# Small products set singly between 512-column products, fillers at the start, and spatial weights fetched behind VectorE

## The chip, the cores and the metric

The kernel runs on one core of one Trainium2 chip. Its metric is device time in microseconds (us), the median of several executions. A core has TensorE (PE, the 128x128 matmul array, which writes to PSUM), VectorE (DVE), ScalarE (ACT), GpSimd (POOL) and SyncE (SP); here SP and POOL mostly issue DMAs, each in the order of its queue. A PE product is two steps, a weight load (PEld: the stationary operand, 128 columns here) and the matmul (the moving operand, up to 512 columns). A transpose is a product with the identity.

## The reference, cut to what matters

```python
# SEQ 256, D 2048, two layers, all float32; rms_norm before every sub-layer, plain residual adds
z = gelu(h @ w_in); u, v = split(z)                      # layer 0: spatial gating, chunks of 128 tokens
v = rms_norm(v, g_v).reshape(..., CHUNK, 16 heads, 128)
s = einsum('hts,bcshd->bcthd', tril(w_s), v) + b_s
h = h + (u * s) @ w_out
u = h @ w_in                                             # layer 1: S5, 128 heads of 16 channels, 64 states
x_t = abar * x_{t-1} + bbar @ u_t                        # complex diagonal scan over the chunk
y = c @ x (real part) + d * u
ga, gb = split(gelu(y) @ w_glu); h = h + ga * sigmoid(gb)
# after each of the two: gated MLP, hidden 5632
z = causal_conv3(h @ w_up) + conv_b; gate, val = split(z)
h = h + (silu(gate) * val) @ w_down
```

## The kernel before, in words

All 256 tokens stay on chip: `hn` holds the residual stream, and the weights (about 400 MB) are streamed once. Each weight tile (1 MB) comes by a DMA of SP into one of three raw buffers. ACT rounds it to a high part (`wh`, L124), DVE takes the difference (`wl`, L125), and the activations are split in the same way, so that each fp32 product is made of three: high by high, high by low, low by high. Each of them is 512 columns wide in the two forms that hold most of the work, `group_b` (L893 to L895, into `accb`) and `form_b` (L987 to L989, into `accv`). `form_a` makes a pair of 512 and 256 columns (L786 and L787, into `acc`).

Between these stand small products of 128 columns or less, all on PE:
- `stage_pair` (L821, `pt`): four transposes bring a pair of 128-channel chunks of the residual into `X`, the moving or stationary operand of the next layer. `residual` and `glu_evac` put such calls on a list, `pending`, and `drain` takes one from it after each weight tile.
- `activate` in the gated MLP (L916, `zt`): four transposes per chunk of 128 hidden units, then convolution, silu and product on ACT and DVE, into `Gt`. These calls go through `pending` too; there are 88 of them, 352 transposes.
- `spatial_weights` (L1089, `ps_w`) and `spatial` (L1108, `ps_s`) in the spatial gating; `wr` and `bb_` are the spatial weights and biases, loaded by POOL (L1084, L1086).
- S5 (16 groups of heads): `drive` (L584, `ps_x`), then the rotation by a table (`tab`, loaded by SP, doubled by ACT at L566), the scan and the rotation back on ACT and DVE, then `outputs` (`ps_y`: 4 products at L639 from the input, 8 at L645 from the scan's result `sp`), `gelu` on ACT (L653, `y`). One step of each is issued after each weight tile, in an order by slots (`sched`, `step`).
- The preparation of S5's constants runs in the background of the first gated MLP, some instructions after each tile (`bg`, `ps_k` at L458).

These products go through two PSUM buffers of one pool (`misc`). At the start PE runs 7 products of ones (`warm`, L1041) while the input comes.

A scheduler of the language lays the program's instructions out on the engines, by a modelled timeline: it may move an instruction behind later ones of its engine. So the order on PE is not quite the order of the code. `issue_after(ins)` is a context that keeps the instructions issued in it behind `ins` on `ins`'s engine.

Of the kernel before, what the change touches and what calls it, by code (L numbers as in the profile page):

```python
# [66 lines left out]

N_WARM = 7

BG_OUT = (1.0, 1.0, 1.0, 0)  # L70
# [446 lines left out]
class S5Tokens:  # L517
# [61 lines left out]
    def drive(self, s):  # L579

        st = self.st[s]
        st["x"] = self.psum.tile([P, 512], F32, name=f"ps_x{s}", tag="misc")
        for i in range(4):
            self.nc.tensor.matmul(  # L584
                st["x"][:, i * P : (i + 1) * P], st["pw"][:, i, :], st["ubd"][:, i, :], start=True, stop=True
            )

    def take(self, s):
# [80 lines left out]
def tile_hybrid_trunk(  # L669
# [101 lines left out]
    def form_a_steps(Xt, nks, blocks, evac, k0=0):  # L771

        pairs = [acc_ps.tile([P, 2, 512], F32, name="acc", tag="acc") for _ in range(len(blocks) // 2)]
        k_first, ktot = k0, k0 + sum(nks)
        for nk in nks:
            part = ws.get()  # L780
            for b, c0 in enumerate(blocks):
                ps = pairs[b // 2][:, b % 2, :]
                for kk in range(nk):
                    k = k0 + kk
                    wh, wl = part(kk, c0, P)
                    T.matmul(ps, wh, Xt[k], start=k == k_first, stop=False, skip_group_check=True)  # L786
                    T.matmul(ps[:, NT:], wl, Xt[k][:, :NT], start=False, stop=k == ktot - 1, skip_group_check=True)  # L787
                if k0 + nk == ktot and b % 2 == 1:
                    evac(b // 2, pairs[b // 2])
            k0 += nk  # L790
            yield
# [19 lines left out]

    def stage_pair(i, g_col, pool=None):

        if pool is None:
            pt = misc_ps.tile([P, 512], F32, name="pt", tag="misc")
        else:
            pt = pool.tile([P, 2, 512], F32, name="pt", tag="acc")[:, 0, :]
        for j in range(2):
            for a in range(2):
                c = 2 * i + j  # L820
                T.transpose(pt[:, j * NT + a * P : j * NT + (a + 1) * P], hn[:, a, c * P : (c + 1) * P], ident)  # L821
        for j in range(2):
            stage_x(2 * i + j, g_col, pt[:, j * NT : (j + 1) * NT])
# [24 lines left out]
    rb2 = bcast(rbc, 2, 1)  # L848
    pending = []

    def drain(n=1):

        while pending and n > 0:
            pending.pop(0)()
            n -= 1

    def residual(tp, g, ps, g_col=None):
# [3 lines left out]
        if g_col is not None:  # L861
            for a in range(2):
                square_sum(tp, hv[:, a, :], nss[:, a, g : g + 1])
            for i in (2 * g, 2 * g + 1):
                pending.append(lambda i=i: stage_pair(i, g_col))
            if g == 3:
# [11 lines left out]
    def group_b_steps(Xt, nks, evac, after=None, k0=0):  # L878
# [6 lines left out]
        for ti, nk in enumerate(nks):  # L885
            part = ws.get()
            for kk in range(nk):
                k = k0 + kk
                wh, wl = part(kk, 0, 512)
                for tt in range(2):  # L890
# [3 lines left out]
                    T.matmul(ps[:, tt, :], xh, wl, start=False, stop=False)  # L894
                    T.matmul(ps[:, tt, :], xl, wh, start=False, stop=k == ktot - 1)  # L895
            k0 += nk
            if k0 == ktot:
                evac(ps)
            drain()
            if after is not None and ti in after:  # L900
# [7 lines left out]
    def ffn(l, g_next, fin=None):  # L908
        cw = conv

        def activate(z, c, q, k):

            pt = misc_ps.tile([P, 512], F32, name="zt", tag="misc")
            for v in range(2):
                for tt in range(2):
                    T.transpose(  # L916
                        pt[:, v * NT + tt * P : v * NT + (tt + 1) * P],
                        z[:, tt, v * NT + q * P : v * NT + (q + 1) * P], ident,
                    )
            a = fpool.tile([P, 2, NT], F32, name="a", tag="a", bufs=2)  # L920
            for v in range(2):
# [55 lines left out]
    def form_b_steps(Xt, nks, pss, own=0, between=None):  # L977
# [15 lines left out]
        for k, (get, kk) in enumerate(chunks):  # L993
            part = get() if get else part
            w = part(kk, 0, 512)
            product(k, w, 0)
            if k < ktot - own:
                product(k, w, 1)
            else:
                kept.append((k, w))  # L1000
# [7 lines left out]
    with ExitStack() as sgu_ctx:  # L1008
# [35 lines left out]
        stage_pair(0, cols[:, 0], acc_ps)  # L1044
        ws.split(0)
        stage_pair(1, cols[:, 0], acc_ps)
        pss = acc_ps.tile([P, 2, 512], F32, name="accv", tag="acc")
        first_v = form_b_steps(X, [4] * 4, [pss[:, tt, :] for tt in range(2)])
        for i in range(2, 8):
            stage_pair(i, cols[:, 0])  # L1050
# [7 lines left out]
        total_r(vss, 4, rtok)  # L1058


        for g in range(4):
# [17 lines left out]
        for g in range(4):  # L1079
            st = {}  # L1080

            def spatial_weights(g=g, st=st):
                wr = sp.tile([P, 4, P], F32, name="wr", tag="wr", bufs=2)
                nc.gpsimd.dma_start(wr, a_w_s[0][4 * g : 4 * g + 4].rearrange("h t s -> t h s"))  # L1084
                st["b"] = sp.tile([P, 4, P], F32, name="bb_", tag="bb_", bufs=2)
                nc.gpsimd.dma_start(st["b"], dram(a_b_s, g * 512, [[0, P], [1, 512]]).rearrange("p (h t) -> p h t", h=4))  # L1086
                ps = misc_ps.tile([P, 512], F32, name="ps_w", tag="misc")
                for i in range(4):
                    T.transpose(ps[:, i * P : (i + 1) * P], wr[:, i, :], ident)  # L1089
                w = st["w"] = sp.tile([P, 4, P], F32, name="wst", tag="wst", bufs=2)  # L1090
                A.copy(w.rearrange("s h t -> s (h t)"), ps)
# [11 lines left out]
            def spatial(p, st=st, g=g):  # L1103
                ps = misc_ps.tile([P, 512], F32, name="ps_s", tag="misc")
                for i in range(2):
                    hd = 4 * g + 2 * p + i
                    for a in range(2):
                        T.matmul(  # L1108
                            ps[:, i * NT + a * P : i * NT + (a + 1) * P],
                            vn[:, a, hd * P : (hd + 1) * P], st["w"][:, 2 * p + i, :], start=True, stop=True,  # L1110
                        )
                s = sp.tile([P, 2, 2, P], F32, name="s_", tag="s_", bufs=3)
                for i in range(2):
# [17 lines left out]
            def first(g=g):  # L1131
                if g == 0:
                    make_rbc(sp)
                spatial_weights()
# [26 lines left out]
    with tc.tile_pool(name="s5", bufs=1) as sp:  # L1161
# [17 lines left out]
        for s in range(KC):  # L1179
            n = N_OF[s]  # L1180
            at(n - 1, s5.load, s)
            at(n - 1, s5.load1, s)
            at(n, s5.drive, s)
            at(n + 1, s5.take, s)
# [7 lines left out]
        order = (  # L1192
            s5.gelu, s5.take, s5.finish, s5.fetch, s5.turn, s5.scan, s5.outputs, s5.drive, s5.load2, s5.load, s5.load1
        )

        n_slot = [0]

        def step():
            for fn, a in sorted(sched.pop(n_slot[0], []), key=lambda e: order.index(e[0])):
                fn(*a)  # L1200
# [32 lines left out]
        def glu_evac(i):  # L1233
            def evac(ps):
                for a in range(2):
# [6 lines left out]
                    square_sum(sp, hv, nss[:, a, i // 2 : i // 2 + 1])  # L1242
                pending.append(lambda: stage_pair(i // 2, cols[:, 3]))
                if i == KC - 2:
# [12 lines left out]
        for i in range(4, KC, 2):  # L1257
            group_b(Ys, [4, 4], glu_keep(i), {0: step, 1: step})
        assert not sched
        craw = fetch_conv(sp, 1)  # L1260
# [71 lines left out]
```

## Time and profile before

| | |
|---|---|
| time, median of 3 runs | 2111.91 us (2110.3 to 2114.04) |
| the profiled execution: its own time, its span | 2112.45 us, 2110.7 us |
| PE busy, weight loads busy | 2092.9 us (99%), 1734.2 us (82%) |
| DVE, ACT, POOL busy | 1438.0, 1151.5, 90.4 us |
| mean granted clock of TensorE | 0.998 |
| HBM read | 410.47 MB, 205 GB/s over the span |

The span runs from the first to the last instruction. Rows of PE's products are as long as the product is in flight; products overlap, so what one costs is the step from its start to the next one's. The stages on the time axis: spatial gating to 200 us, its out-projection and the first gated MLP to about 1050, S5 with the GLU to about 1390, the second gated MLP to the end.

### The profile page before, as it was taken

The page shows a single profiled execution, that of the slowest core. Times are in us where ns is not written, and L with a number is a line of the kernel's source. Part 1 is how long each engine was busy: PE and PEld are TensorE (multiplying, and loading weights), DVE is VectorE, ACT ScalarE, POOL GpSimd, SP SyncE. Part 2 cuts the span into 40 slices and gives each one's busy share as a digit, 9 for nine tenths or more (in the row PEclk, how much of TensorE's full clock was granted, in tenths as well). Part 3 has the DMA queues.
Part 4 walks back from the last instruction along what each step waited for, and adds up shares of the span by engine and source line. Part 5 has one row for each costly group of instructions (what it writes and reads, how often), then busy time and mean ns, then how long its engine had stood idle before and what let it go on. Part 6 is the DMA issues. An engine that isn't in the chain of part 4 may idle for free.

```text
span 2110.7 us, 27318 instructions
## 1 busy us (share of the span) xinstructions
PE 2092.9 (99%) x10279; PEld 1734.2 (82%) x10279; DVE 1438.0 (68%) x2123; ACT 1151.5 (55%) x1672; POOL 90.4 (4%) x142
## 2 busy tenths in 40 slices
PE   9999999999999999999999999999999999999998
PEld 7888888888887788888887788888888888888886
DVE  5476777886896644888779867765655666546565
ACT  6544455554555544555468756555544555345553
POOL 1010000000111110000000000000000000000000
PEclk9999999999999999999999999999999999999999
DMA  8655556666777766666789976565556555555553
GB/s 280 198 185 179 183 191 207 210 228 222 220 236 236 222 215 192 192 205 205 232 251 273 280 220 208 189 202 185 182 191 200 180 189 187 188 194 182 192 185 120
DMA packets 356293, 434.39 MB, mean 206 GB/s; under 512 B 31457, under 2 KB 275265, under 8 KB 355521
## 3 DMA queue, kind: packets, MB, share of 16 engines
q1 hardware_dynamic: 346704, 403.75, 59.9%
q0 software_dynamic: 9424, 28.88, 4.6%
q8 instruction: 81, 1.33, 0.3%
q14 instruction: 52, 0.42, 0.1%
q10 hardware_dynamic: 32, 0.01, 0.0%
HBM read 410.47 MB, written 22.02 MB: 205 GB/s over the span
## 4 chain that ended last, share of the span: by engine, by line
PE 90%; DMA 4%; DVE 3%; issue 2%; ACT 1%; SPq 0%; ACTq 0%; POOL 0%; DVEq 0%; POOLq 0%
PE accb L893 25%; PE accb L894 25%; PE accb L895 25%; PE acc L786 3%; PE zt L916 2%; PE acc L787 1%; PE accv L987 1%; PE accv L988 1%; PE accv L989 1%; DMA tab<-rd 1%; DVE wl L125 1%; DMA yt<-yd 1%; PE pt L821 1%; DMA qd<-qt 1%; DMA yd<-y 1%
## 5 line engine op out<-in xcount | busy, mean ns | idle before, releaser
L125 DVE TENSOR_TENSOR wl<-w,wh 128x1024 fp32r<-128x1024 f32 (+1 forms) x721 | 878.6, 1222 | 571.2 <-ACT wh L124 567.2
L124 ACT CAST wh<-w 128x1024 fp32r<-128x1024 f32 (+1 forms) x721 | 753.9, 1050 | 704.0 <-PE accb L895 606.1
L895 PE MATMUL accb<-wh,X 128*128 128x512 f32 x1408 | 552.3, 392 | 0.0
L893 PE MATMUL accb<-wh,X 128*128 128x512 f32 x1408 | 551.7, 392 | 0.0
L894 PE MATMUL accb<-wl,X 128*128 128x512 f32 x1408 | 549.1, 390 | 0.0
L893 PE MATMUL accb<-wh,Gt 128*128 128x512 f32 x1060 | 415.7, 392 | 0.0
L894 PE MATMUL accb<-wl,Gt 128*128 128x512 f32 x1060 | 413.6, 391 | 0.7 <-DVE wl L125 0.7
L895 PE MATMUL accb<-wh,Gt 128*128 128x512 f32 x1060 | 413.8, 391 | 0.0
L895 PEld LDWEIGHTS accb<-wh,X 128*128 128x128 f32 x1408 | 264.3, 188 | 57.0
L894 PEld LDWEIGHTS accb<-wl,X 128*128 128x128 f32 x1408 | 264.5, 188 | 54.5
L893 PEld LDWEIGHTS accb<-wh,X 128*128 128x128 f32 x1408 | 264.4, 188 | 53.8
L894 PEld LDWEIGHTS accb<-wl,Gt 128*128 128x128 f32 x1060 | 199.1, 188 | 42.0 <-DVE wl L125 1.1
L893 PEld LDWEIGHTS accb<-wh,Gt 128*128 128x128 f32 x1060 | 199.0, 188 | 41.9 <-issue 0.3
L895 PEld LDWEIGHTS accb<-wh,Gt 128*128 128x128 f32 x1060 | 199.0, 188 | 41.4
L786 PE MATMUL acc<-X,wh 128*128 128x512 f32 x512 | 184.6, 402 | 0.0
L787 PE MATMUL acc<-X,wl 128*128 128x256 f32 x512 | 144.9, 283 | 0.0
L786 PEld LDWEIGHTS acc<-X,wh 128*128 128x128 f32 x512 | 96.5, 189 | 22.6 <-issue 0.9
L924 ACT ACTIVATE a<-zt,conv 128x256 f32<-128x256 f32 x176 | 94.3, 557 | 14.9 <-PE zt L916 8.1
L787 PEld LDWEIGHTS acc<-X,wl 128*128 128x128 f32 x512 | 97.1, 190 | 0.6 <-issue 0.2
L943 ACT ACTIVATE z<-accb,rtok 128x512 f32<-128x512 f32 x88 | 55.8, 685 | 65.9 <-PE accb L895 65.9
L925 DVE SCALAR_TENSOR_TENSOR a<-zt,conv,a 128x255 f32<-128x255 f32 x176 | 77.7, 476 | 13.7 <-ACT a L924 13.7
L928 DVE SCALAR_TENSOR_TENSOR a<-zt,conv,a 128x254 f32<-128x254 f32 x176 | 77.1, 474 | 0.7
(300 smaller groups left out, 1423.8 us busy)
## 6 DMA issues: line engine op xcount, KB each, us to landing
w<-in_f_w_up_dram SPq DMA_DIRECT2D x352, 512.0 KB, 4.6
w<-in_f_w_down_dram SPq DMA_DIRECT2D x80, 1024.0 KB, 5.2
w<-in_b_w_glu_dram SPq DMA_DIRECT2D x64, 512.0 KB, 4.8
w<-in_a_w_in_dram SPq DMA_DIRECT2D x28, 1024.0 KB, 5.2
w<-in_a_w_out_dram SPq DMA_DIRECT2D x16, 1024.0 KB, 5.1
w<-in_b_w_in_dram SPq DMA_DIRECT2D x16, 1024.0 KB, 6.5
w<-in_f_w_down_dram SPq DMA_DIRECT2D x16, 512.0 KB, 3.7
qd<-qt POOLq DMA_DIRECT2D x16, 320.0 KB, 5.2
```

The costliest lines, as they stand in the source:

```text
L124: self.nc.scalar.copy(hi[:, a:b], raw[:, o + a : o + b])
L125: self.nc.vector.tensor_tensor(lo[:, a:b], raw[:, o + a : o + b], hi[:, a:b].bitcast(F32), op=ALU.subtract)
L786: T.matmul(ps, wh, Xt[k], start=k == k_first, stop=False, skip_group_check=True)
L787: T.matmul(ps[:, NT:], wl, Xt[k][:, :NT], start=False, stop=k == ktot - 1, skip_group_check=True)
L893: T.matmul(ps[:, tt, :], xh, wh, start=k == k_first, stop=False)
L894: T.matmul(ps[:, tt, :], xh, wl, start=False, stop=False)
L895: T.matmul(ps[:, tt, :], xl, wh, start=False, stop=k == ktot - 1)
L916: T.transpose(pt[:, v * NT + tt * P : v * NT + (tt + 1) * P], z[:, tt, v * NT + q * P : v * NT + (q + 1) * P], ident,)
L924: A.activation(a[:, v], zt, AF.Identity, bias=cw[:, 3, cv : cv + 1], scale=cw[:, 2, cv : cv + 1])
L925: V.scalar_tensor_tensor(a[:, v, 1:], zt[:, : NT - 1], cw[:, 1, cv : cv + 1], a[:, v, 1:], ALU.mult, ALU.add)
L928: V.scalar_tensor_tensor(a[:, v, 2:], zt[:, : NT - 2], cw[:, 0, cv : cv + 1], a[:, v, 2:], ALU.mult, ALU.add)
L943: A.mul(z[:, tt], ps[:, tt], rtok[:, tt : tt + 1])
```

## The change

`activate`, `stage_pair`, `spatial_weights`, `spatial` and `drive` become generators that yield after each small product. `weave` puts such a generator on a list, and `tick`, called after each three products of 512 columns (in `form_b` twice, in `form_a` after each pair), runs it to its next yield. `settle` runs all that is on the list. `drain` is replaced in `group_b` by `resume`, which weaves one pending call, ahead of `evac`. Six products of ones (N_BRIDGE) are set between the first and the second group of the input's transposes. The spatial weights' loads of groups 0 and 1 move to the loop before, under `issue_after(last_on_vector())`.

```diff
+N_BRIDGE = 6
@@ drive
                 st["x"][:, i * P : (i + 1) * P], st["pw"][:, i, :], st["ubd"][:, i, :], start=True, stop=True
             )
+            yield
@@ form_a_steps
                     T.matmul(ps[:, NT:], wl, Xt[k][:, :NT], start=False, stop=k == ktot - 1, skip_group_check=True)
+                    tick()
@@ stage_pair
-    def stage_pair(i, g_col, pool=None):
+    def stage_pair(*args):
+        for _ in stage_pair_steps(*args):
+            pass
+
+    def stage_pair_steps(i, g_col, pool=None):
...
                 T.transpose(pt[:, j * NT + a * P : j * NT + (a + 1) * P], hn[:, a, c * P : (c + 1) * P], ident)
+                yield
@@ 
-    pending = []
+    pending, woven = [], []
+
+    def weave(steps):
+
+        woven.append(steps)
+
+    def tick():
+
+        while woven:
+            if next(woven[0], woven) is not woven:
+                return
+            woven.pop(0)
+
+    def settle():
+        while woven:
+            tick()
 
     def drain(n=1):
 
+        settle()
         while pending and n > 0:
-            pending.pop(0)()
+            for _ in pending.pop(0)():
+                pass
             n -= 1
+
+    def resume():
+
+        settle()
+        if pending:
+            weave(pending.pop(0)())
@@ group_b_steps
                     T.matmul(ps[:, tt, :], xl, wh, start=False, stop=k == ktot - 1)
+                    tick()
             k0 += nk
+            resume()
             if k0 == ktot:
                 evac(ps)
-            drain()
@@ activate
                         z[:, tt, v * NT + q * P : v * NT + (q + 1) * P], ident,
                     )
+                    yield
@@ form_b_steps
             product(k, w, 0)
+            tick()
+            tick()
@@ the start
         ws.split(0)
+        with tc.issue_after(next(i for i in reversed(nc.cur_bb.bb.instructions) if i.engine == mybir.EngineType.PE)):
+            for i in range(N_BRIDGE):
+                T.matmul(warm[:, :P], ones, ones, start=True, stop=True)
         stage_pair(1, cols[:, 0], acc_ps)
...
+        def fetch_spatial(g):
+            st = spatial_of[g]
+            st["wr"] = sp.tile([P, 4, P], F32, name="wr", tag="wr", bufs=2)
+            nc.gpsimd.dma_start(st["wr"], a_w_s[0][4 * g : 4 * g + 4].rearrange("h t s -> t h s"))
+            st["b"] = sp.tile([P, 4, P], F32, name="bb_", tag="bb_", bufs=2)
+            nc.gpsimd.dma_start(st["b"], dram(a_b_s, g * 512, [[0, P], [1, 512]]).rearrange("p (h t) -> p h t", h=4))
...
+            if g > 1:
+                with tc.issue_after(last_on_vector()):
+                    fetch_spatial(g - 2)
...
-                {0: first, 1: lambda: spatial(0), 2: lambda: spatial(1)},
+                {
+                    0: first, 1: lambda: (settle(), weave(spatial(0))),
+                    2: lambda: (settle(), weave(spatial(1))),
+                },
@@ S5
+        def drive(s):
+            weave(s5.drive(s))
...
         def step():
+            settle()
```

How this lays out the instructions, at three places. First PE in an up-projection of the first gated MLP; `zt` are the transposes, `accb` the 512-column products. Before:

```order
L893 MATMUL accb<-wh_3135,X_2036 128x512
L894 MATMUL accb<-wl_3136,X_2036 128x512
L916 MATMUL zt<-ident,z 128x128
L895 MATMUL accb<-wh_3135,X_2036 128x512
L916 MATMUL zt<-ident,z 128x128 x7
L893 MATMUL accb<-wh_3139,X_2182 128x512
L894 MATMUL accb<-wl_3140,X_2182 128x512
```

Now:

```order
L949 MATMUL zt<-ident,z 128x128
L925 MATMUL accb<-wh_2961,X_2255 128x512
L926 MATMUL accb<-wl_2962,X_2255 128x512
L927 MATMUL accb<-wh_2961,X_2255 128x512
L949 MATMUL zt<-ident,z 128x128
L925 MATMUL accb<-wh_2961,X_2258 128x512
L926 MATMUL accb<-wl_2962,X_2258 128x512
L927 MATMUL accb<-wh_2961,X_2258 128x512
L949 MATMUL zt<-ident,z 128x128
```

Eight transposes of two chunks stood together, but for one product; now each stands alone behind three products, in two runs of four. In the whole program 325 of the 352 stand so, where 43 stood alone before.

Second, S5. PE before, at the fifth group's outputs (`ps_y`; its fp32 products run as two passes each, so the trace counts twice as many):

```order
L639 MATMUL ps_y_9810<-ubd_8918,tw_9633 64x128 x4
L786 MATMUL acc<-X_8408,wh_9647 128x512
L787 MATMUL acc<-X_8408,wl_9648 128x256
L786 MATMUL acc<-X_8411,wh_9647 128x512
L787 MATMUL acc<-X_8411,wl_9648 128x256
L786 MATMUL acc<-X_8450,wh_9647 128x512
L787 MATMUL acc<-X_8450,wl_9648 128x256
L786 MATMUL acc<-X_8453,wh_9647 128x512
L787 MATMUL acc<-X_8453,wl_9648 128x256
L786 MATMUL acc<-X_8581,wh_9737 128x512
L645 MATMUL ps_y_9810<-sp_8926,qw_9631 64x64 x8
```

and now:

```order
L642 MATMUL ps_y_9816<-ubd_8913,tw_9634 64x128 x4
L648 MATMUL ps_y_9816<-sp_8921,qw_9632 64x64 x8
L789 MATMUL acc<-X_8471,wh_9648 128x512
L790 MATMUL acc<-X_8471,wl_9649 128x256
L586 MATMUL ps_x_9854<-ubd_8919,pw_9733 128x128
L789 MATMUL acc<-X_8474,wh_9648 128x512
L790 MATMUL acc<-X_8474,wl_9649 128x256
L586 MATMUL ps_x_9854<-ubd_8919,pw_9733 128x128
```

The two parts of ps_y stood apart in 10 of the 16 groups and do so in 2 now; ps_x stands singly. SP there, around the table load of group 6, before and now:

```order
L551 DMA ubd_8922<-ud 64x4x64 x2
L108 DMA w_9651<-in_b_w_in_dram 128x8x256
L574 DMA qw_9631<-qd 128x640
L556 DMA pw_9732<-pd 128x4x128
L655 DMA yd<-y_9685 64x4x64 x2
L565 DMA tab_9639<-rd 64x2x512
```

```order
L553 DMA ubd_8917<-ud 64x4x64
L576 DMA qw_9632<-qd 128x640
L553 DMA ubd_8917<-ud 64x4x64
L567 DMA tab_9640<-rd 64x2x512
L110 DMA w_9652<-in_b_w_in_dram 128x8x256
L658 DMA yd<-y_9691 64x4x64 x2
```

The table's load stood behind the weight tile's and the output's (`yd`), which waits for ACT's `y`; now it stands ahead of both.

Third, POOL at the start, with the semaphores that a row waits for. Before, and now:

```order
L1054 DMA gains<-in_a_g_v_dram 16x128
L1084 DMA wr<-in_a_w_s_dram 128x4x128
L1086 DMA bb__936<-in_a_b_s_dram 128x512
L1084 DMA wr<-in_a_w_s_dram 128x4x128
L1086 DMA bb__1161<-in_a_b_s_dram 128x512
L963 DMA craw_717<-in_f_conv_w_dram 88x3x128 [waits DMASW0_49,Activation_49]
```

```order
L1094 DMA gains<-in_a_g_v_dram 16x128
L1106 DMA wr<-in_a_w_s_dram 128x4x128
L1108 DMA bb__725<-in_a_b_s_dram 128x512
L1106 DMA wr<-in_a_w_s_dram 128x4x128
L1108 DMA bb__881<-in_a_b_s_dram 128x512
L997 DMA craw_727<-in_f_conv_w_dram 88x3x128 [waits DMASW0_49,Activation_49]
```

The spatial weights' loads keep their place, and none of the four waits for a semaphore.

## Rows read from the trace of the kernel before

**Rows 1.** The page's first part: busy time, share of the span, instructions.
```profile
PE 2092.9 (99%) x10279; PEld 1734.2 (82%) x10279; DVE 1438.0 (68%) x2123; ACT 1151.5 (55%) x1672; POOL 90.4 (4%) x142
```

**Rows 2.** Timeline of PE, 317.2 to 322.7 us: start, duration, operation, count.
```profile
317.25 0.39 PE L895 MATMUL accb<-wh,X 128*128 128x512 f32 x1
...
318.38 0.40 PE L894 MATMUL accb<-wl,X 128*128 128x512 f32 x1
318.62 0.27 PE L916 MATMUL zt<-ident,z 128*128 128x128 f32 x1
318.65 0.48 PE L895 MATMUL accb<-wh,X 128*128 128x512 f32 x1
318.97 0.93 PE L916 MATMUL zt<-ident,z 128*128 128x128 f32 x7
...
322.69 0.39 PE L894 MATMUL accb<-wl,X 128*128 128x512 f32 x1
```

**Rows 3.** Timeline of PE, 347.6 to 351.5 us.
```profile
347.61 0.40 PE L894 MATMUL accb<-wl,X 128*128 128x512 f32 x1
347.84 0.60 PE L916 MATMUL zt<-ident,z 128*128 128x128 f32 x4
...
351.50 0.39 PE L894 MATMUL accb<-wl,X 128*128 128x512 f32 x1
```

**Rows 4.** Timeline of PE, 1302.8 to 1304.2 us.
```profile
1302.86 0.39 PE L895 MATMUL accb<-wh,Gt 128*128 128x512 f32 x1
1303.09 0.27 PE L821 MATMUL pt<-ident,hn 128*128 128x128 f32 x1
1303.11 0.48 PE L893 MATMUL accb<-wh,Gt 128*128 128x512 f32 x1
...
1303.89 0.40 PE L893 MATMUL accb<-wh,Gt 128*128 128x512 f32 x1
1304.13 0.40 PE L894 MATMUL accb<-wl,Gt 128*128 128x512 f32 x1
```

**Rows 5.** Two stretches: busy time per engine, granted clock, DMA share, GB/s.
```profile
1100.00:1170.00 70.00, 67.10 (x506) 54.83 (x502) 64.35 (x88) 56.20 (x81) 3.78 (x7) 0.98 0.98 273
1133.20:1136.60 3.40, 3.40 (x24) 2.59 (x23) 1.53 (x2) 1.14 (x2) 0.00 (x0) 0.50 1.07 362
```

**Rows 6.** Timeline of the start, PE, its weight loads (PEld) and POOL.
```profile
1.20 3.06 PEld L1041 LDWEIGHTS warm<-ones 128*128 128x128 f32 x14 [1.20 <-POOL ones L733]
...
3.83 0.80 POOL L1084 DMA_DIRECT2D wr<-in_a_w_s_dram  x1
...
7.74 1.12 PE L821 MATMUL pt<-ident,hn 128*128 128x128 f32 x4 [1.92 <-DMA hn<-in_x_dram]
...
11.21 0.63 PE L987 MATMUL accv<-wh,X 128*128 128x512 f32 x1
...
11.64 0.63 PE L988 MATMUL accv<-wl,X 128*128 128x512 f32 x1
```

**Rows 7.** Timeline of PE in S5, 1181.1 to 1183.7 and 1209.0 to 1210.8 us.
```profile
1181.16 0.39 PE L894 MATMUL accb<-wl,Gt 128*128 128x512 f32 x1
1181.48 0.69 PE L645 MATMUL ps_y<-sp,qw 128*64 128x64 f32 x16
...
1182.76 0.66 PE L639 MATMUL ps_y<-ubd,tw 128*64 128x128 f32 x8
...
1183.68 0.40 PE L895 MATMUL accb<-wh,Gt 128*128 128x512 f32 x1
...
1209.06 0.39 PE L895 MATMUL accb<-wh,Gt 128*128 128x512 f32 x1
1209.38 0.66 PE L639 MATMUL ps_y<-ubd,tw 128*64 128x128 f32 x8
1209.87 0.64 PE L645 MATMUL ps_y<-sp,qw 128*64 128x64 f32 x16
...
1210.77 0.39 PE L894 MATMUL accb<-wl,Gt 128*128 128x512 f32 x1
```

**Rows 8.** Timeline of ACT, 1130 to 1132 us.
```profile
1130.60 1.04 ACT L566 COPY tab<-tab 64x1024 f32<-64x1024 f32 x1 [2.80 <-DMA tab<-rd]
1131.67 0.38 ACT L653 ACTIVATE y<-ps_y 128x256 f32<-128x256 f32 x1
```

More of the change, by code (lines that the diff above doesn't have):

```diff
@@ L864, in residual @@
             for i in (2 * g, 2 * g + 1):
-                pending.append(lambda i=i: stage_pair(i, g_col))
+                pending.append(lambda i=i: stage_pair_steps(i, g_col))
             if g == 3:
@@ L1049, in tile_hybrid_trunk @@
         for i in range(2, 8):
-            stage_pair(i, cols[:, 0])
+            weave(stage_pair_steps(i, cols[:, 0]))
             next(first_v)
             next(first_v)
+            settle()
         for i, src in enumerate((norm_ffn_g[0], norm_mix_g[1], norm_ffn_g[1], a_g_v[0])):
@@ L1058, in tile_hybrid_trunk @@
         total_r(vss, 4, rtok)
+        spatial_of = [{} for _ in range(4)]
+        def fetch_spatial(g):
[4 more added lines that the diff above has]
+            nc.gpsimd.dma_start(st["b"], dram(a_b_s, g * 512, [[0, P], [1, 512]]).rearrange("p (h t) -> p h t", h=4))
         for g in range(4):
@@ L1079, in tile_hybrid_trunk @@
         for g in range(4):
-            st = {}
+            st = spatial_of[g]
             def spatial_weights(g=g, st=st):
[L1083 to L1086, printed above, removed]
+                if g > 1:
+                    fetch_spatial(g)
+                wr = st["wr"]
                 ps = misc_ps.tile([P, 512], F32, name="ps_w", tag="misc")
@@ L1089, in spatial_weights @@
                     T.transpose(ps[:, i * P : (i + 1) * P], wr[:, i, :], ident)
+                    yield
                 w = st["w"] = sp.tile([P, 4, P], F32, name="wst", tag="wst", bufs=2)
@@ L1111, in spatial @@
                         )
+                        yield
                 s = sp.tile([P, 2, 2, P], F32, name="s_", tag="s_", bufs=3)
@@ L1133, in first @@
                     make_rbc(sp)
-                spatial_weights()
+                weave(spatial_weights())
                 scale_v()
@@ L1182, in tile_hybrid_trunk @@
             at(n - 1, s5.load1, s)
-            at(n, s5.drive, s)
+            at(n, drive, s)
             at(n + 1, s5.take, s)
@@ L1192, in tile_hybrid_trunk @@
         order = (
-            s5.gelu, s5.take, s5.finish, s5.fetch, s5.turn, s5.scan, s5.outputs, s5.drive, s5.load2, s5.load, s5.load1
+            s5.gelu, s5.take, s5.finish, s5.fetch, s5.turn, s5.scan, s5.outputs, drive, s5.load2, s5.load, s5.load1
         )
@@ L1198, in step @@
         def step():
+            settle()
             for fn, a in sorted(sched.pop(n_slot[0], []), key=lambda e: order.index(e[0])):
@@ L1242, in evac @@
                     square_sum(sp, hv, nss[:, a, i // 2 : i // 2 + 1])
-                pending.append(lambda: stage_pair(i // 2, cols[:, 3]))
+                pending.append(lambda: stage_pair_steps(i // 2, cols[:, 3]))
                 if i == KC - 2:
@@ L1258, in tile_hybrid_trunk @@
             group_b(Ys, [4, 4], glu_keep(i), {0: step, 1: step})
+        settle()
         assert not sched
```

## The prediction

> **What bounds the kernel now.** I read the busy shares first, then the waits by stretch, then TensorE's (PE's) queue product by product where the change touches it. PE's matmul row is busy 99% of the span [rows 1], so the only things worth counting are what one instruction more or less costs in PE's queue, and the few places where PE does not run. Undisturbed, 512-column products start 0.2267 us apart: five of them lie between 317.25 and 318.38 us [rows 2]. A row's printed length (0.39) is longer than that step because the products overlap; the step between starts is the price.
>
> PE's stops are few. At the start it waits 1.92 us for the input, and until about 13.6 us products start 0.43 apart (11.21 to 11.64) instead of 0.23: TensorE's lower level, 1.2 of 2.4 GHz [rows 6]. In the S5 stage, between 1100 and 1170 us, PE is busy 67.1 of 70 us, VectorE (DVE) 64.35 of 70, and the DMA share is 0.98; for 3.4 us of it the granted clock is 0.50 [rows 5]. Everywhere else PE's own order is the time.
>
> **Part 1: transposes singly.** What does a 128-column transpose cost in a group and alone? Subtract 0.2267 for each 512-column product in a stretch; the rest is the transposes' price, with all they do to the products behind them.
> - Eight, as one, a product and seven [rows 2]: from 318.38 to 322.69 us is 4.31 us and holds 15 products, 3.40. The rest is 0.91, so 0.114 each, or 0.455 for four.
> - Four in a row [rows 3]: from 347.61 to 351.50 us is 3.89 us with 15 products. The rest is 0.49, so 0.12 each.
> - One alone [rows 4], the only clean one: from 1302.86 to 1303.89 us is 1.03 us with 4 products, 0.907. The rest is 0.123. Read one product further, to 1304.13, it is 1.27 less 5 products, 0.137.
>
> So one alone isn't cheaper. In a row, one starts 0.11 after the other, about twice the quarter of 0.2267 that its 128 columns would take; and after the one that stands alone the next product still comes late, although 512 columns run on either side. Products after any such interruption also start 0.229 to 0.235 apart for about ten steps, and alone, every third product, each interruption gets its share of that.
>
> From the order of instructions: in the gated MLPs 325 of 352 transposes (zt) now stand alone, each with three products to the next; before, 43 did, 38 of these one product ahead of seven others. An interruption in every three products costs 0.123, and the last of four leaves about 0.02 behind in the products after it: 4 x 0.123 + 0.02 = 0.51 per four. Against half an eight (0.455) that is 0.055 more, for 76 fours: +4.2 us. Against a lone four (0.49) it is 0.02, for 5: +0.1. The input's transposes (pt), the spatial weights' and the spatial and S5 products now stand alone in 55, 12, 27 and 55 cases, about 38 fours; no row shows them alone but the one above, so I take 0.04, between 0.02 and 0.055: +1.5. Sum **+5.8 us**. Bounds: 0, if one alone costs what a member of eight does (0.114), and 119 fours x (4 x 0.137 - 0.455) = +11.
>
> Does a transpose that now ends 2 us later hold anything up? By the order, the shortest way from the last transpose of a hidden chunk to the first product that reads its result is 42 products in the changed kernel, 9.6 us at 0.2267, where it was 41. That is room for a chain of some ten half-microsecond instructions on ScalarE (ACT) and DVE: nothing.
>
> **Part 2: the S5 products (ps_y), and the waits around them.** This is a move that the diff doesn't name: since the small products now stand elsewhere, the scheduler sets the two parts of ps_y (4 and 8 products) next to each other. Before, 10 of 16 were split; now 2 are. Split: 1181.16 to 1183.68 us is 2.52 us with 4 products, so 1.61 for both parts. Joined: 1209.06 to 1210.77 us is 1.71 with 2 products, 1.26 [rows 7]. Eight joins are worth 8 x 0.35 = -2.8. One group of the background products (ps_k) more than before costs the same once: **+0.3**.
>
> But all eight lie in the S5 stage's densest stretch, between about 1110 and 1170 us, where DVE has only 70 - 64.35 = 5.65 us to spare in 70 and DMA less [rows 5]. There PE waits: 2.9 us idle, and 3.4 us at half clock, which cost 1.7. The largest wait starts on ACT: a copy of the rotation table waits 2.80 us for its DMA and the activation that frees PE's PSUM buffer stands behind it, so it comes only at 1131.67 [rows 8]. In the new order of SP the loads of tables 6 to 9 stand ahead of the weight loads that they followed, so this wait can go. Joins and waits together promise 2.8 + 4.6 = 7.4 us, and DVE lets at most 5.65 through in that stretch. On the other side, a joined ps_y asks for the scan's result at once, where its second part used to come 9 products later or more; if each of the 8 waits half a microsecond, it is +4. I take half of what DVE lets through: **-2.8**.
>
> **Part 3: the start.** Twelve passes more of 128 columns (six fp32 products, two passes each) stand between the first and the second group of transposes. At 3.06/14 = 0.22 us each [rows 6] that is 2.6 us from about 5.55 us on, to 8.15, where the second group began at 7.74: +0.4. In exchange PE has no idle stretch. If its clock rises earlier for that, the products between 8.5 and 13.6 us start 0.23 instead of 0.43 apart, worth at most 2.5 if the weights keep up. Bounds -2.5 and +0.4; I take the middle, **-1.0**.
>
> **Part 4: the spatial weights.** They are not fetched later. GpSimd (POOL) issues the DMAs of the first two groups at 3.83 us [rows 6] behind the gains' loads; in the new order the four rows stand at the same place and wait for nothing. The dependence is put on instructions of DVE's engine, and a DMA issue of POOL isn't one: 0, and the DMA load at the start stays as it is.
>
> **Sum:** 5.8 + 0.3 - 2.8 - 1.0 = +2.3 us on the profiled execution's 2112.45, so 2114.8. That execution lies 0.54 above the median of the runs shown (2111.91); against the median I forecast **2114.2 us**.
>
> **Rivals.** What this measurement can tell from no change is 0.2%, 4.2 us.
> - *Slower: each one alone costs 0.13 or more.* Place: the gated MLPs, outside any wait, so nothing hides it. Price: at 0.137 part 1 is +11 and the total +7.5: 2119.4 us. It decides from about 0.132, where the sum passes +4.2. For it: the same single transpose, read one product further. Against it: the eight of rows 2, whose first stands alone and makes the whole no dearer.
> - *Faster: the S5 stage gives all that DVE lets through, and one alone costs 0.114.* 0 + 0.3 - 5.65 - 1.0 = -6.3: about 2105.6 us. For it: tables fetched earlier on SP. [...]
> - *Much faster: the 512-column products hide the transposes' weight loads, and the transposes no longer hold up the products.* Then one alone costs its columns, a quarter of 0.2267, 0.057: 119 fours x (0.227 - 0.455) = -27, in all -30.5: about 2081 us. For it: each of the products beside it lasts twice as long as a transpose's 0.11. The Trainium skill (TensorE: Matmul & The Clock Gate, Step-by-step: what each phase is for) says that a weight load is pulled ahead of matmuls in flight, into a background buffer, so that a long product covers the load of what comes next. The trace agrees only for the load of the transpose itself; the load of the product behind it has just the short transpose to hide under. Against it, from the trace: 0.123 for the one that stands alone [rows 4], not 0.057.
>
> **How the numbers follow.** Forecast 0.53; slower rival 0.32; faster 0.10; much faster 0.05. The forecast's own range is 2107.7 to 2116.1, and it is the class of no difference. Leaving out the much faster case and the ends of the other two gives 2106 to 2121 us. Faster by over 0.2%: 0.10 + 0.05 = 0.15; within 0.2%: 0.53; slower: 0.32.
>
> **What would show it.** In the changed profile, three products and one transpose in an up-projection should take 0.80 us (3 x 0.2267 + 0.123); 0.74 would make the much faster rival right, over 0.81 the slower one. The first gated MLP with its 44 fours should grow by about 44 x 0.055 = 2.4 us. In the S5 stage PE's wait for y should go and some wait at the second part of ps_y (for the scan's result or its weights) should come. At the start, products should reach a step of 0.23 before 13.6 us, and POOL should issue the spatial weights at about 3.8 us as before; a later issue would prove part 4 wrong. A time under 2106 or over 2121 means that a term is missing, most likely in the S5 stage.

## The result, and where the time went

The changed kernel takes 2122.48 us (median of 4 runs, 2120.11 to 2127.72) against 2112.39 of the kernel before: ratio 1.0056, 95% interval 1.0039 to 1.0073. It is slower, by about 10 us; the forecast was 2114.2 in a range up to 2121. The profiled execution is the shortest of the four, 2120.11 us with a span of 2118.4, so its profile shows 7.7 us of the loss; the other three had a mean granted clock of 0.996 to 0.997 where this one had 0.999.

The first part of the page after, as in [rows 1]:

```profile
PE 2094.8 (99%) x10291; PEld 1718.9 (81%) x10291; DVE 1454.4 (69%) x2123; ACT 1150.1 (54%) x1672; POOL 90.1 (4%) x142
```

PE is as busy as before, and its share says nothing. What says something is a clock that both kernels carry: the 8,896 large products (512 or 256 columns) stand in the same order in both queues, but for 26 that change places with near ones between the 4504th and the 4547th. The start of product N in one timeline less its start in the other is the shift up to there, and the growth of the shift from one N to the next is what a stretch cost. The marks N are set where both queues have the same small products behind them; one product later, at 4961, the joined ps_y is behind the mark in one queue and ahead of it in the other, and the shift reads 1.1 us more. All tables here are made so, each from one profiled execution, against the profile before (us):

| stretch, by product number | before lasts | after | forecast |
|---|---|---|---|
| start, to 201 | 59.8 | +0.69 | -1.0 |
| values, spatial, projection, 201 to 1341 | 245.4 | +0.91 | |
| first gated MLP, 1341 to 4448 | 741.5 | +2.31 | +2.4 |
| entry of S5, 4448 to 4578 | 24.3 | -0.17 | |
| S5 first part, 4578 to 4960 | 95.6 | **+2.77** | -2.8 with the rows beside it |
| S5 second part, 4960 to 5450 | 129.7 | -1.60 | |
| second MLP, 5450 to the last | 804.9 | +2.79 | |
| sum | | +7.7 | +2.3 |

The two MLPs and the row of +0.91 make 6.0 us; part 1 of the forecast was 5.8, with the ps_k term 6.1.

**The MLPs.** PE's timeline after, an up-projection:

```profile
344.72 0.27 PE L949 MATMUL zt<-ident,z 128*128 128x128 f32 x1
...
345.54 0.27 PE L949 MATMUL zt<-ident,z 128*128 128x128 f32 x1
...
346.34 0.27 PE L949 MATMUL zt<-ident,z 128*128 128x128 f32 x1
...
347.14 0.27 PE L949 MATMUL zt<-ident,z 128*128 128x128 f32 x1
...
347.95 0.40 PE L925 MATMUL accb<-wh,X 128*128 128x512 f32 x1
```

From one transpose to the next there are 0.82, 0.80 and 0.80 us: three products and one transpose, as forecast. Over the 111 places of the first MLP where two lone transposes stand so, the mean is 0.804. The four cost 347.95 - 344.72 - 12 x 0.2267 = 0.51 us, where half an eight cost 0.455 [rows 2]. The long products beside them make them no cheaper. The weight loads of the first of these steps:

```profile
344.72 0.19 PEld L925 LDWEIGHTS accb<-wh,X 128*128 128x128 f32 x1
344.83 0.19 PEld L926 LDWEIGHTS accb<-wl,X 128*128 128x128 f32 x1
345.07 0.19 PEld L927 LDWEIGHTS accb<-wh,X 128*128 128x128 f32 x1
```

The load of the product behind the transpose starts together with the transpose, and the next load 0.11 us later, not 0.057.

**The start.** PE after, and then POOL's issue of the spatial weights:

```profile
4.98 1.50 PE L1084 MATMUL warm<-ones 128*128 128x128 f32 x12
7.61 0.65 PE L829 MATMUL pt<-ident,hn 128*128 128x128 f32 x4 [1.13 <-DMA hn<-in_x_dram]
...
9.03 0.39 PE L1022 MATMUL accv<-wl,X 128*128 128x512 f32 x1
9.25 0.40 PE L1023 MATMUL accv<-wh,X 128*128 128x512 f32 x1
...
15.79 0.41 PE L829 MATMUL pt<-ident,hn 128*128 128x128 f32 x2 [2.73 <-DMA hn<-in_x_dram]
```

```profile
3.82 0.78 POOL L1106 DMA_DIRECT2D wr<-in_a_w_s_dram  x1
```

Products start 0.22 apart from 9 us on, where they were 0.43 apart at 11 [rows 6]: the filler did what it was put there for, and product 10 starts 2.81 us earlier than before. Then PE waits 2.73 us for the input, and by product 100 the start is 0.69 us behind. The spatial weights are issued at 3.82 as before at 3.83 [rows 6].

**The S5 stage.** First the windows from product 4578 to 4960, before and after (length, then busy time of PE, weight loads, DVE, ACT and POOL, then granted clock, DMA share, GB/s); then PE's waits in them, before (1070 to 1167 us) and after (1078 to 1174 us; total, number, longest); then PE's and ACT's timelines at two places:

```profile
1070.97:1166.55 95.58, 92.41 (x663) 77.07 (x662) 86.11 (x115) 69.60 (x99) 3.78 (x7) 0.98 0.97 271
```

```profile
1074.70:1173.05 98.35, 89.67 (x664) 76.07 (x662) 87.00 (x116) 71.33 (x101) 3.78 (x7) 1.00 0.95 265
```

```profile
PE ps_y L639 <- ACT y L653: 2.3, 2, 1.9
PE ps_x L584 <- DVE q L599: 0.5, 1, 0.5
PE ps_x L584 <- DMA ubd<-ud: 0.3, 1, 0.3
```

```profile
PE ps_x L586 <- DMA ubd<-ud: 3.4, 3, 2.0
PE ps_x L586 <- DVE q L602: 2.3, 2, 1.5
PE ps_x L586 <- DVE u L1274: 1.3, 1, 1.3
PE ps_x L586 <- ACT y L656: 0.9, 1, 0.9
PE ps_y L642 <- ACT y L656: 0.4, 1, 0.4
```

```profile
1145.07 0.66 PE L642 MATMUL ps_y<-ubd,tw 128*64 128x128 f32 x8
1145.56 0.64 PE L648 MATMUL ps_y<-sp,qw 128*64 128x64 f32 x16
1146.12 0.50 PE L789 MATMUL acc<-X,wh 128*128 128x512 f32 x1
1146.46 0.28 PE L790 MATMUL acc<-X,wl 128*128 128x256 f32 x1
1148.70 0.46 PE L586 MATMUL ps_x<-ubd,pw 128*128 128x128 f32 x2 [1.96 <-DMA ubd<-ud]
```

```profile
1130.27 1.05 ACT L568 COPY tab<-tab 64x1024 f32<-64x1024 f32 x1 [0.68 <-DMA tab<-rd]
1131.34 2.00 ACT L126 CAST wh<-w 128x1024 fp32r<-128x1024 f32 x2
1133.24 0.37 ACT L656 ACTIVATE y<-ps_y 128x256 f32<-128x256 f32 x1
```

The copy of the table waits 0.68 us instead of 2.80 [rows 8], and PE's wait for y at ps_y falls from 2.3 to 0.4 us, as forecast; the clock does not fall here. (ACT's waits for all table loads of the stretch hardly change, 8.2 us before and 7.5 now; they moved.) For the same products PE is busy 89.67 us instead of 92.41, so 2.7 of the 4.5 us that the joins and the clock promised were there. But it is idle 98.35 - 89.67 = 8.7 us instead of 3.2. DVE, which was to be the limit, is busy 87.00 of 98.35 us, a smaller share than before. The waits now stand at ps_x, the input products of the next token step. After ps_y come two large products (a pair of form_a), and then ps_x: it asks for its PSUM buffer and its blocks (ubd) at the very start of a step, and the other large products are queued behind it. In the order before, its row stood 10 to 23 large products behind the first part of ps_y (the six groups from 1113 to 1158 us).

### The profile page after: what moved, and what is told of

Its sections match the earlier page's. It is cut to its first block, busy times and chain, and to the rows that moved or that the text cites. A ratio compares the mean times of both kernels' runs of the same rounds, so it can differ in the third digit from the quotient of the medians.

```text
span 2118.4 us, 27362 instructions
## 1 busy us (share of the span) xinstructions
PE 2094.8 (99%) x10291; PEld 1718.9 (81%) x10291; DVE 1454.4 (69%) x2123; ACT 1150.1 (54%) x1672; POOL 90.1 (4%) x142
## 4 chain that ended last, share of the span: by engine, by line
PE 93%; DMA 3%; DVE 2%; issue 1%; ACT 1%; SPq 0%; ACTq 0%; DVEq 0%; POOLq 0%
PE accb L925 27%; PE accb L927 26%; PE accb L926 26%; PE acc L789 3%; PE zt L949 2%; PE acc L790 2%; PE accv L1023 1%; PE accv L1021 1%; PE accv L1022 1%; DMA tab<-rd 1%; DMA yd<-y 1%; PE pt L829 1%; DMA hn<-in_x_dram 1%; DMA yt<-yd 1%; DVE wl L127 0%
## 5 line engine op out<-in xcount | busy, mean ns | idle before, releaser
L925 PE MATMUL accb<-wh,X 128*128 128x512 f32 x1408 | 575.5, 409 | 0.0
L927 PE MATMUL accb<-wh,X 128*128 128x512 f32 x1408 | 551.0, 392 | 0.0
L789 PE MATMUL acc<-X,wh 128*128 128x512 f32 x512 | 190.9, 411 | 0.0
L949 PE MATMUL zt<-ident,z 128*128 128x128 f32 x352 | 92.5, 272 | 0.0
L959 DVE SCALAR_TENSOR_TENSOR a<-zt,conv,a 128x255 f32<-128x255 f32 x176 | 83.9, 477 | 6.9 <-ACT a L958 6.9
L962 DVE SCALAR_TENSOR_TENSOR a<-zt,conv,a 128x254 f32<-128x254 f32 x176 | 84.4, 480 | 4.1
```

What stands on the lines that cost most here:

```text
L925: T.matmul(ps[:, tt, :], xh, wh, start=k == k_first, stop=False)
L949: T.transpose(pt[:, v * NT + tt * P : v * NT + (tt + 1) * P], z[:, tt, v * NT + q * P : v * NT + (q + 1) * P], ident,)
L959: V.scalar_tensor_tensor(a[:, v, 1:], zt[:, : NT - 1], cw[:, 1, cv : cv + 1], a[:, v, 1:], ALU.mult, ALU.add)
L962: V.scalar_tensor_tensor(a[:, v, 2:], zt[:, : NT - 2], cw[:, 0, cv : cv + 1], a[:, v, 2:], ALU.mult, ALU.add)
```

## The experiments

### The MLPs' transposes back in rows

Run rows, on the changed kernel:

```diff
-            resume()
             if k0 == ktot:
                 evac(ps)
+            drain()
```

> The changed kernel with one edit: the transposes of the gated MLPs and of the stages behind them are issued in a row again after each weight tile, as before; the bridge at the start and the single products in the spatial and S5 stages stay. Theory A (one alone costs 0.014 us more per transpose, as the step 0.80 for three products and one says): part 1 gives back about 5 us. The scheduler's order in the S5 stage turns back with it (ps_y split in 9 of 16, ps_x in rows well behind it), so the stage's 2 to 4 us come back too; total 2113 to 2116 us. Theory B (the interleaving in the MLPs costs nothing and the S5 stage alone holds the loss): the MLP stages keep their times product by product, total 2117 to 2119 us.

Measured 2116.08 us, ratio to before 1.0027 (1.0017 to 1.0036). By products, the first MLP costs +0.20 and the second 0.00 where the changed kernel has +2.31 and +2.79: so much for the transposes alone, and theory A's 5 us hold. The S5 code is still the changed one, with its ps_x handed out singly, yet the scheduler's order there is again that of before, with ps_y in two parts and ps_x in rows behind the second, and the first part of S5 costs -1.5. The order that hurts is a side effect of the change in the MLPs. The profiled execution took 2110.98 us and the eleven others 2113.64 to 2119.99, so the median lies above the expected range and the profile below it; what those others lost, no trace shows.

### What ps_x waits for

Three runs on the changed kernel: ps_x at once in a row (s5_row), five pairs of products later (s5_late), and with the blocks of the step before, so that it waits for no transfer (s5_old).

```diff
-            weave(s5.drive(s))
+            for _ in s5.drive(s): pass      # s5_row
+            weave(later(s5.drive(s)))       # s5_late: five empty steps ahead
...
-    st["pw"][:, i, :], st["ubd"][:, i, :],
+    st["pw"][:, i, :], self.ubd[(s - 1) % 4][:, i, :],   # s5_old
```

> The changed kernel with one edit: the four input products of an S5 token step (ps_x) are issued in a row again, at once. By its instruction order the two parts of ps_y stay joined and the row of ps_x now stands directly behind them, where the changed kernel has two products between. Theory A (PE waits at the first ps_x because it stands right behind ps_y, before the data and the PSUM buffer are there): the wait stays or grows by the 0.35 us of the two products missing, the S5 stage gains nothing, total 2121 to 2125 us against 2122.5. Theory B (issuing the ps_x singly is what costs the stage its time): the S5 stage gets back what it lost, 1.6 to 4 us, total 2118 to 2121 us.

> The changed kernel with one edit: the first ps_x of an S5 step is issued five products later than in the changed kernel. By its order ps_y is split into 4 and 8 again in 10 of 16 groups, and most ps_x stand 12 products and more behind ps_y. Theory A: PE's waits at ps_x (10.5 us in the changed kernel's profile) fall below 4 us, half at least of which is kept; the splits cost 8 x 0.35 = 2.8 us back; total 2116 to 2120 us. Theory B (DVE or the DMAs bound the stage, and waits only move): the waits come back at ps_y or elsewhere, total 2121 to 2125 us.

> The changed kernel, in which the input products of an S5 step (ps_x) read the input blocks (ubd) of the step before instead of their own, so the results are not the reference's; loads, products and their number stay, and the order in the S5 stage stays y joined with ps_x two products behind. Theory A (the transfer of ubd, issued 6 to 8 us before, ends last when ps_x stands at the start of a step): PE's waits at ps_x fall from 10.5 us to under 4, the stage gives back 4 us or more, total 2116 to 2119 us. Theory B (the wait is for the PSUM buffer, which ACT and DVE free by reading the step before): the waits stay 8 us and more under the names y and q, total 2121 to 2125 us.

| run | us | ratio (interval) | S5 first part | S5 second part |
|---|---|---|---|---|
| after | 2122.48 | 1.0056 (1.0039 to 1.0073) | +2.77 | -1.60 |
| s5_row | 2123.56 | 1.0059 (1.0044 to 1.0074) | +3.54 | -2.78 |
| s5_late | 2128.50 | 1.0085 (1.0071 to 1.0099) | +3.64 | +4.68 |
| s5_old | 2127.65 | 1.0069 (1.0055 to 1.0083) | +5.80 | +2.08 |

s5_row came as theory A said: a row in the same place takes nothing back. s5_late is a miss, above both ranges. The scheduler set the other products anew around the later ps_x and PE waited at ps_y and, in the second part, for the scan. s5_old, above both ranges too, is a miss for the transfer as the cause. PE's waits in its first part:

```profile
PE ps_y L648 <- DVE sp L628: 3.6, 1, 3.6
PE ps_x L586 <- DVE q L602: 2.8, 4, 1.5
PE ps_y L642 <- ACT y L656: 1.9, 1, 1.9
PE ps_y L642 <- DVE q L602: 1.4, 1, 1.4
```

No row names ubd any more, and PE waits no less (the mean granted clock was also lower there, 0.95 against 1.00, which is part of the +5.80). My reading, argued and not shown, is that whatever ends last, the next one is right behind it: the order makes all the inputs of a step due at one point.

### The order of S5 alone

To separate that order from all else, PE's order in the first part of S5 was written out and fixed: an order like that of before, more regular, put into the changed kernel (spread2), and the order of the changed kernel put into the one before (b_joined2). Three earlier runs with the same aim (spread, b_joined, best: 2136.61, 2138.72, 2127.37 us) had the first part of ps_y traced behind the load that refills its blocks; it waited for that load and read the blocks of a later step, so they tell nothing of the order.

In the slots, a half is one of the two large products of a form_a pair.

```diff
+    tc.keep_in_program_order(T.matmul(...))   # every large product and ps_x, ps_y here
...
+    slot of spread2:    ps_y part 1; 14 halves; ps_y part 2; 4 halves; ps_x x4
+    slot of b_joined2:  ps_y; 2 halves; ps_x; 2 halves; ps_x; ...
```

> The run named spread once more, with the first four products of ps_y traced ahead of the load that refills their input blocks (in the three runs before this they stood behind it, read the blocks of a later step and waited for its load). The changed kernel with PE's order in the S5 stage's first part written out and fixed: four products of ps_y at the start of a step, the eight others 14 half products later, the ps_x in a row 4 behind those. Theory A (what the S5 stage lost, it lost by its order): it gives back 3 to 5 us, total 2117 to 2119.5 us where the changed kernel has 2122.5. Theory B (it loses because DVE, ACT and the DMAs come too late in any order): 2121 us and more.

> The run named b_joined once more with the same mend. The kernel before with PE's order in the S5 stage's first part written out and fixed as the changed kernel has it: ps_y joined at the start of a step, the four ps_x singly behind it, two half products between; all else as before. Theory A (the order alone costs it): 3 to 5 us slower than before, 2113.5 to 2116 us where before has 2110 to 2111. Theory B (it is no loss by itself): 2108 to 2111.5 us.

The totals mislead: 2133.39 us (1.0099, 1.0085 to 1.0113) and 2127.29 (1.007, 1.0056 to 1.0084). By products:

| run | S5 order | entry, 4448 to 4578 | first part, 4578 to 4960 | of that part, PE idle |
|---|---|---|---|---|
| before | spread | 0 | 0 | 3.2 |
| rows, b_bridge, b_late, b_both | spread | 0.0 | -1.5, -1.3, -1.3, -1.3 | 2.9, 3.7, 3.5, 3.6 |
| spread2 (MLPs changed) | spread, fixed | +9.3 | **+0.6** | 4.7 |
| after, s5_row, late | joined | -0.2 | +2.8, +3.5, +5.1 | 8.7, 10.8, 10.2 |
| b_joined2 (MLPs as before) | joined, fixed | +9.1 | **+5.9** | 8.0 |

The windows of b_joined2 and of spread2 from product 4578 to 4960:

```profile
1079.47:1180.99 101.52, 93.56 (x663) 80.22 (x662) 87.35 (x115) 71.92 (x103) 3.77 (x7) 0.95 0.89 251
```

```profile
1085.35:1181.51 96.16, 91.49 (x664) 77.00 (x662) 84.14 (x113) 70.64 (x99) 3.24 (x6) 0.98 0.92 260
```

PE's waits in that part, of b_joined2 and then of spread2:

```profile
PE ps_x L584 <- DVE q L600: 4.6, 3, 2.1
PE ps_x L584 <- DMA ubd<-ud: 2.3, 2, 2.0
PE ps_x L584 <- DVE x L601: 0.6, 1, 0.6
PE ps_y L640 <- ACT y L655: 0.5, 1, 0.5
```

```profile
PE ps_x L586 <- ACT tab L568: 3.7, 1, 3.7
PE ps_x L586 <- ACT Gt L1230: 0.9, 1, 0.9
```

The loss goes with the order in both directions, whatever the MLPs do: with the joined order the kernel before is idle 8.0 us there instead of 3.2 and loses 5.9, some of it at the lower clock (0.95 against 0.98), and with the spread order the changed kernel is idle 4.7 us instead of 8.7 and loses 0.6. Both fixed runs enter the stage some 9 us late, so the timing of the entry is not what parts them. What is shown for this stretch is the stage's order as a whole, not PE's alone: SP's queue went with it. In spread2 SP issues yd, yd, pw, tab, tw, ubd, ubd, w, w, qw from step to step, as the kernel before does, and in b_joined2 tw, ubd, qw, ubd, tab, w, w, yd, yd, pw, as the changed one does. No run has one of the two queues without the other.

The whole-kernel times carry another cost that I had not foreseen: fixing the order holds large products of S5 behind the last transposes and behind ps_r, the product that spreads the norm's factor, for which PE waits. PE's timeline of spread2 there:

```profile
1057.70 1.03 PE L835 MATMUL pt<-ident,hn 128*128 128x128 f32 x8
1065.09 1.20 PE L860 MATMUL ps_r<-dg,ones 128*128 128x128 f32 x4 [6.36 <-issue]
```

With that wait of 6.36 us the granted clock falls to 0.50 for 6.8 us (1063.9 to 1070.7), which costs about half of the 5.6 us that PE runs in them; the two make up the entry's 9.3, and it is why neither total came out as expected. Where the fixing ends, in the second part, spread2 lost another 2.6 us. So over the whole stage nothing was won back. That part varies by itself, too: with one and the same spread order it cost -2.1 in the profiles of b_bridge and b_both and +5.3 in that of b_late.

### The start

On the changed kernel (late): the first two groups of spatial weights really fetched later. On the kernel before: the bridge alone (b_bridge), the later fetch alone (b_late) and both (b_both). The order of S5 is that of their base in all four.

```diff
+    if g < 2:                                                # late, b_late, b_both
+        G.tensor_copy(wr[:, 0, 0:1], vss[:, 0, g : g + 1])   # and the biases alike
     nc.gpsimd.dma_start(wr, ...)
...
+    for i in range(6):                                       # b_bridge, b_both
+        T.matmul(warm[:, :P], ones, ones, start=True, stop=True)
     stage_pair(1, cols[:, 0], acc_ps)
```

> The changed kernel with one edit: the first two groups of the spatial weights and biases are really fetched later, because GpSimd writes one column of each tile from a sum of the first or second value group before their DMA. PE's order is the same. Theory A (with the bridge the start is bound by the DMAs that bring the input, 8 x 256 KB behind which 1.05 MB of spatial weights and biases take their share): at some 370 GB/s the 1.05 MB are 2.8 us, of which the waits of 2.73 and 0.56 us for the input at 12 to 19 us give back 2 to 3 us; total 2119.5 to 2121 us. Theory B (the input waits for its own queue, in which three loads are issued within 5 us): the waits stay, total 2122 to 2124 us.

> The kernel before with one edit: the six products of ones between the first two groups of input transposes. Every other order stays. Theory A (the input's transfers bound the start): the granted clock rises before 9 us instead of at 13.6, PE gains some 2.5 us by its tenth product and loses them by its twentieth in waits for the input; total the same as before to within 1 us, +0.3 to +0.7 in the profile. Theory B (the forecast's): PE keeps 0.9 us of it, total 2111 where before is 2112.

> The kernel before with one edit: the first two groups of spatial weights and biases are really fetched later (GpSimd writes one column of each tile from a sum of the first or second value group before their DMA). Theory A: the input comes earlier, but PE at its lower level does not need it earlier, so the start keeps its time to within 0.5 us. Theory B (PE's first wait of 1.92 us is for a transfer that shares the bandwidth too): it falls and with it the start, by 0.5 to 1 us.

> The kernel before with both edits, bridge and really later spatial weights. Theory A (two limits one behind the other: first the clock, then the input's transfers, and each edit alone takes away one): the start is 1.3 to 2.6 us shorter than before, total 2108 to 2110 us where before is 2110 to 2112. Theory B (each works for itself): the sum of what the two alone give, some 0.5 us.

| run | us | ratio (interval) | start, to 201 |
|---|---|---|---|
| late | 2120.30 | 1.0045 (1.0032 to 1.0059) | -1.37 |
| b_bridge | 2113.41 | 1.0011 (1.0002 to 1.0021) | +3.77 |
| b_late | 2110.47 | 0.9993 (0.9984 to 1.0001) | -1.29 |
| b_both | 2109.23 | 0.9984 (0.9975 to 0.9993) | -1.18 |

(At product 100 the runs with the later fetch still have four products of ps_g ahead of them that the others have done; at 201 all have.) PE at the third and fourth group of input transposes, first b_bridge, then b_both:

```profile
12.71 0.66 PE L821 MATMUL pt<-ident,hn 128*128 128x128 f32 x4 [1.32 <-DMA hn<-in_x_dram]
...
16.23 0.63 PE L821 MATMUL pt<-ident,hn 128*128 128x128 f32 x4 [0.55 <-DMA hn<-in_x_dram]
...
18.52 0.63 PE L989 MATMUL accv<-wh,X 128*128 128x512 f32 x1 [0.58 <-DVE X L808]
18.96 0.63 PE L987 MATMUL accv<-wh,X 128*128 128x512 f32 x1
```

```profile
11.11 0.60 PE L821 MATMUL pt<-ident,hn 128*128 128x128 f32 x4
...
13.86 0.60 PE L821 MATMUL pt<-ident,hn 128*128 128x128 f32 x4
...
15.18 0.50 PE L989 MATMUL accv<-wh,X 128*128 128x512 f32 x1 [0.25 <-DVE X L808]
```

With the bridge alone PE runs into the input's transfers; after these stops the products are 0.44 apart again (18.52 to 18.96). It cost more than theory A said: 3.8 us in the profile and 2.1 in the median. With 1.05 MB less in the queues, the transposes of b_both wait for nothing. For late the start gives back 0.69 + 1.37 = 2.06 us, the lower end of theory A; by their intervals the times of late and after can't be told apart. b_late is a miss: its start is 1.29 us shorter, more than either theory said, but there the clock, too, stood higher in part of the start than in the profile before, and its median is not told from before. So of the two limits one behind the other only a part is borne out: the bridge without the later fetch costs, with it the kernel is faster than before. That the bridge adds anything to the later fetch is not shown, as b_late's start is as short as b_both's and the intervals of their times overlap. **b_both is the fastest of the kernels here**: 2109.23 us, about 2 us below the kernel before.

A last run put the spread, fixed S5 order on top of it (best2):

> The run named best once more with the same mend: the kernel before with the bridge, the really later spatial weights, and the spread S5 order written out and fixed. Theory A (a regular spread order waits no more than the scheduler's): 2107 to 2110 us. Theory B (a fixed order takes from PE the freedom to go round a late transfer): 2111 to 2114 us.

It took 2124.17 us (1.0055, 1.0042 to 1.0068), above both ranges: +11.2 at the entry, +1.0 in the first part, +3.0 in the second. The fixing costs more than there was to win.

## Why the prediction was wrong, by its own steps

- *Part 1, singles, +5.8*: right. 2.31 + 2.79 + 0.91 = 6.0 us by products, 0.51 for four, 2.31 for the first MLP where 2.4 was forecast; undone, the MLPs' part is gone (rows). The much faster rival falls with it: with a long product on either side, a transpose still costs about 0.12 and not 0.057. The Trainium skill's rule named there (TensorE: Matmul & The Clock Gate, Step-by-step: what each phase is for) is a weight load pulled ahead of the matmuls in flight. The trace agrees for the load that stands behind a long product, 0.23 us ahead of its own product; the load behind the short one starts with the transpose at 344.72, and the 0.80 us per three products and a transpose fit a load that the transpose can't cover. That this is the reason for the price is argued; no run varied it. The slower rival's side is where the time came out, but not for its reason: one alone costs 0.127 and not 0.137. (By its own formula it would have decided from 0.130, not 0.132. And the tail of about ten slower products stands behind fours; behind the eight of [rows 2] only two steps, 0.233 and 0.231, are slower.)
- *Part 2, S5, -2.8*: this step failed. It priced the joins of ps_y (0.35 each) and the wait for y, and took "half of what DVE lets through". Both gains came in part: PE is busy 2.7 us less in the first part. The new wait was looked for at the second part of ps_y, with up to +4; it came at ps_x, whose place two large products behind the joined ps_y stood in the order and was not weighed. PE's idle time in the first part rose by 5.5 us, and that part lost 2.8 us (2.8 to 5.9 in the four profiles with that order and its own blocks); with its entry and second part S5 came out at +1.0. The bound from DVE's idle share was never reached: DVE's busy share fell from 0.90 to 0.88.
- *Part 3, the start, -1.0*: wrong in sign, by the same kind of mistake. The clock rose early and the gain of 2.8 us by product 10 was there; "if the weights keep up" was the condition, and the input did not: +0.69 here, +0.32 to +3.77 in the profiles with the bridge and the early fetch.
- *Part 4, the spatial weights, 0*: right, they are issued at 3.82 us. What the words of the change promise was worth 2.06 us in the profile of late.
- *Sum*: between the forecast's +2.3 and the profile's +7.7 lie 5.4 us. S5 with its entry came out at +1.0 and not -2.8, 3.8 of them; the start at +0.7 and not -1.0, 1.7; part 1 and the ps_k term, 6.0 together, came out 0.1 lower. The other 2.4 us of the median lie in executions without a trace. Their lower mean granted clock fits to more half-speed stretches such as the 3.4 us that cost 1.7 [rows 5]; that is argued, not shown.

## What to carry to other kernels

Don't count on long products to hide a short one between them: here a lone 128-column transpose cost 0.12 us, no less than one in a group; price one interruption in the trace before spreading hundreds. Where a scheduler sets the order, compare the order of every stage, also of those that the diff doesn't touch, and ask of each product that moved forward, not only of those that wait now, when its inputs and its buffer come. To compare two orders by product number, set the marks where both have done the same work. An idle stretch that is filled gives nothing if a transfer ends just behind it, as in b_bridge: look for the second limit first.

## What was not expected of the hardware

The clock's rise at the start is not fixed by PE's order alone. Before it came at 13.6 us; b_late has the same order of PE up to there, and its windows at the start (PE, weight loads, DVE, ACT, POOL busy, then granted clock) show the upper level from 5.1 us on, and the lower again right after PE's wait of 2.15 us for the input:

```profile
5.10:8.40 3.30, 1.15 (x10) 0.86 (x8) 1.78 (x3) 1.78 (x5) 0.00 (x0) 1.00 0.88 298
8.50:11.80 3.30, 3.30 (x11) 2.64 (x10) 2.43 (x4) 2.08 (x4) 0.00 (x0) 0.50 1.07 387
11.90:15.00 3.10, 3.10 (x17) 2.57 (x16) 1.82 (x3) 2.72 (x4) 0.00 (x0) 1.00 1.05 368
```

By my estimate from these stretches (3.3 us at 0.50 cost about 1.7), the start's price in one profile is good to a microsecond or two either way, and a forecast of it should carry that in its range.
